# A two-layer hybrid block on one core: the dt projection as fp32 matmuls in four column groups, the row of norm factors built later, eleven warm-up matmuls for nine

## The chip, the cores and the metric

The kernel runs on one core of a Trainium2 chip. The metric is the time of one execution in microseconds (us), the median of several. PE is TensorE (PEld its weight loads), DVE is VectorE, ACT is ScalarE, POOL is GpSimd, SP is the engine that issues most DMAs.

## The reference

Two layers work on x, [256 tokens, 1024]. Each layer norms x, multiplies it by an input matrix, and runs three branches (a gated spatial mixer, a state space scan, a differential attention) that are gated, merged and projected; a feed forward part follows. What matters here is the norm and the small product `ssm_dt`, 16 columns of the input matrix:

```python
h = rmsnorm(x, attn_norm_g[layer])          # x / rms(x) by token, times a gain by feature
proj = h @ w_in[layer]
gm_u, gm_v, ssm_z, ssm_xbc, ssm_dt, da_q, da_k, da_v, gates = split_cols(proj, IN_SIZES)
...
dt = softplus(ssm_dt.astype(float32) + dt_bias.astype(float32))   # [256, 16]
```

dt sets the decays of the scan, so it is needed with full fp32 precision.

## The kernel before

x stays in SBUF as `x_sb`, features on partitions: 8 tiles of [128 features, 256 tokens], fp32. The gain is multiplied in at once (`scaled_tile`, L353), and the result is kept as two parts in the fp32r format, `h_hi` and `h_lo`. The factor of a token, 1 / rms, is applied later to what the products give. All large weights come as one stream of blocks [128, 2048] (`raw`, 1 MB); each half block is split into `whi` (ACT, L231) and `wlo` (DVE, L234), up to four halves ahead of use (`AHEAD`). Each product is three matmuls (`mm3`, L274): high by high, high by low, low by high. Products with 512 output columns go through `tok_group` (L302; q, k, v, the spatial gate, z, the branch gates), products with features on partitions through `feat_half` (L280; x B C, u, and the feed forward). The items follow each other in the order of `MIX`, q first, then k, then x4, x5 (the pairs of tiles of B and C) and so on.

Beside the stream run generators that `tick` (L257) advances, once for each half block. Two of them matter here:

- `norm_factors` (L366) squares x, sums over features with matmuls against ones (`an_ss`, L382), takes the inverse root on POOL (`an_r`, `an_rp`, L322 and L324), then spreads the factors along a row with matmuls against the identity (`an_rb`, L389) and copies that row to `an_row` (L393). `an_rp` (by token on partitions) scales q and k (L443) and others; `an_row` is first used for x4 (`normed`, L678). The layer finishes this generator between q and k (L449).
- `dt_raw` (L466) multiplies h by the 16 dt columns. The weights are kept as `ws`, [128, 8 tiles, 128 columns] in fp32r: 16 columns of high parts, 16 of low parts, 96 of zeros. `layer_constants` (L404) makes it: a memset on POOL (L419), a DMA from SP that waits for the memset (L420), a copy on ACT (L422), a subtraction on DVE (L423). Sixteen matmuls (L470) take `h_hi` and `h_lo` of the 8 tiles as the moving operand and give `pd`; rows 0 to 31 of it are copied to `dT` (L472) and turned by two matmuls with a stacked identity (`pdt`, L477), which add the two halves.

A scheduler sets the order in which the instructions of an engine stand; each engine runs its own in that order. fp32r matmuls of 128 columns of weights are one instruction with one record of the trace; an fp32 matmul leaves two records, one behind the other. A few bf16 matmuls on zeros (`warm`, L170, nine of them) run before the first data is there.

Of the kernel before, what the change touches and what calls it, by code (L numbers as in the profile page):

```python
# [11 lines left out]
F32 = mybir.dt.float32  # L12
# [18 lines left out]
# order of the mixer's input products: q, k, v, spatial gate g, u, x B C in pairs of tiles, z  # L31
MIX = ("q", "k", "x4", "x5", "v", "x0", "x1", "z0", "x2", "x3", "z1", "g", "u0", "u1")
# buffers of 4 KiB, of 2 KiB and of the split weights
NS4, NS2, NWB, AHEAD = 18, 7, 5, 4
HP = 200
# feed forward: hidden tile after which the down products start
LAG = 5
CUM_WAIT = 6
WARM = 9
# [4 lines left out]
# columns of w_in  # L44
# [3 lines left out]
# row constants of a layer  # L48
R_GMG, R_GMB, R_SSG, R_DTB, R_D, R_QK, R_SUB = 0, 512, 1024, 2048, 2064, 2080, 2208
R_N = 2336  # L50
# per-partition constants of a layer
PC_CW, PC_CB, PC_FW, PC_FB = 0, 48, 60, 60 + 6 * NFT
PC_N = PC_FB + 2 * NFT
# gains of the input norms, per layer: mixer, feed forward
G_N = 16
# constants that depend on shapes alone
# [5 lines left out]
def feat_block(w, c0, c1):  # L62
    """[1024, cols c0:c0+128 and c1:c1+128] -> [128, 2 tiles, 8 k, 128]"""
    a = w.reshape(8, P, -1)
    return np.stack([a[:, :, c : c + P].transpose(1, 0, 2) for c in (c0, c1)], 1).reshape(P, BLK)


def tok_blocks(w):
    """[K, 512 n] -> blocks of [128, 4 k, 512], the k halves of a column group together"""
    k, n = w.shape  # L70
    a = w.reshape(k // 512, 4, P, n // 512, 512).transpose(3, 0, 2, 1, 4)
    return list(a.reshape(-1, P, BLK))


def out_blocks(w):
    """[1024, 1024] -> blocks of [128, 4 tiles, 4 k, 128], halves of k outermost"""
    a = w.reshape(2, 4, P, 2, 4, P).transpose(0, 3, 2, 4, 1, 5)
    return list(a.reshape(-1, P, BLK))
# [41 lines left out]
def bc(ap, n):  # L120
    """append a broadcast dim of n"""
    return ap.unsqueeze(len(ap.shape)).to_broadcast([*ap.shape, n])
# [3 lines left out]
def block_kernel(ctx: ExitStack, tc: tile.TileContext, x, wstream, wdt, rows, prol, pcols, gains, gmw, consts, out):  # L126
# [20 lines left out]
    # the residual stream, features on partitions  # L147
# [13 lines left out]
    # the activation table is there before the data  # L161
# [3 lines left out]
    # the tensor engine's clock is up when the data comes  # L165
# [16 lines left out]
    def prologue():  # L182
        """lambda and -exp(a_log) of both layers"""
        nc.sync.dma_start(pr, prol.rearrange("(o l) f -> o l f", o=1).to_broadcast([P, L, 272]))
        for l in range(L):
            lv = pr[:, l, 0:256].rearrange("p (a b d) -> p a b d", a=2, b=2)
            nc.vector.tensor_tensor(lprod[:, 2 * l : 2 * l + 2, :], lv[:, :, 0, :], lv[:, :, 1, :], op=ALU.mult)
        nc.vector.tensor_reduce(lsum.rearrange("p l a -> p (l a)"), lprod, op=ALU.add, axis=AX.X)
        nc.scalar.activation(lexp, lsum, AF.Exp)
        nc.scalar.activation(aneg, pr[:, :, 256:272], AF.Exp)  # L190
        nc.vector.tensor_scalar(aneg, aneg, -1.0, None, op0=ALU.mult)
        nc.vector.tensor_tensor(neglam, lexp[:, :, 1], lexp[:, :, 0], op=ALU.subtract)
        for l in range(L):
            lam_init = 0.8 - 0.6 * math.exp(-0.3 * l)
            nc.vector.tensor_scalar(neglam[:, l : l + 1], neglam[:, l : l + 1], -lam_init, None, op0=ALU.add)

# [5 lines left out]
    def load_half():  # L202
        i, hf = divmod(stream["i"], 2)
        parts = 1
        if hf == 0:
            raw = wpool.tile([P, BLK], F32, tag="raw", name=f"raw{i}", bufs=3)
            if i == 0:
                # the first block and the tiles of x as they are needed
                for q in range(4):
                    cs = slice(q * 512, (q + 1) * 512)  # L210
                    nc.sync.dma_start(x_sb[:, 2 * q : 2 * q + 2, :], x[:, 2 * q : 2 * q + 2, :])
                    nc.sync.dma_start(raw[:, cs], wstream[i, :, cs])
            elif i == 1:
                for q in range(2):
                    cs = slice(q * HB, (q + 1) * HB)
                    nc.sync.dma_start(raw[:, cs], wstream[i, :, cs])
                nc.sync.dma_start(cst, consts)
            else:
                nc.sync.dma_start(raw, wstream[i])
# [18 lines left out]
    def next_half():  # L238
        """the next half block; those after it are split ahead"""
# [6 lines left out]
    def load_table(name):  # L246
        """the next activations in program order, with their table set in place"""
        table["ins"] = tc.keep_in_program_order(nc.scalar.preload_act_table_set(name)).ins

# [24 lines left out]
    def mm3(o, a_hi, a_lo, b_hi, b_lo, start, stop):  # L274
        """o += a.T @ b, operands as high + low parts of 12 bits"""
# [4 lines left out]
    def feat_half(o, h_hi, h_lo):  # L280
        """one tile of 128 features of h @ w, features on partitions: o [128, 256]"""
# [6 lines left out]
    def feat_pair(o, h_hi, h_lo):  # L288
        """two tiles, with the last features of h as late as can be"""
# [12 lines left out]
    def tok_group(name, act, nk, evac, between=None):  # L302
        """512 columns of a product, tokens on partitions: act(k, i) gives the high and low
        activations of token tile i, evac(i, psum) takes what comes out"""
# [14 lines left out]
    def rsqrt_mean(src, n, scale, name):  # L319
        """(src * scale + eps) ** -0.5"""  # L320
# [15 lines left out]
    def transpose_split(src, dst, name, nk, scale=1.0):  # L336
        """src [128 tokens, nk * 128] -> features on partitions, high and low parts;
        dst(k0, k1) gives where tiles k0 to k1 go"""
# [14 lines left out]
    def scaled_tile(k, g, h_hi, h_lo):  # L353
        """feature tile k of x times its gain, split; the norm's factor of a token is applied to
        what the products give"""
# [10 lines left out]
    def norm_factors(name, res):  # L366
        """1 / rms of x by token: res gets [128, 2] with tokens on partitions, half of it, and the
        same along a row"""
# [17 lines left out]
        yield  # L386
# [7 lines left out]
        rh = sm.tile([P, 2], F32, tag="rhalf", name=f"{name}_rh", bufs=2)  # L394
        nc.vector.tensor_scalar(rh, r[:, 0:2], 0.5, None, op0=ALU.mult)
        res.update(r=r, rh=rh, row=row)
# [7 lines left out]
    def layer_constants(l):  # L404
        if l == 0:
# [12 lines left out]
        wd = s4(f"wd{l}", [P, 8, P])  # L418
        nc.gpsimd.memset(wd, 0.0)  # L419
        nc.sync.dma_start(wd[:, :, 0:HEADS], wdt[l])  # L420
        ws = s4(f"ws{l}", [P, 8, P], F32R)
        nc.scalar.activation(ws, wd, AF.Copy)  # L422
        nc.vector.tensor_tensor(  # L423
            ws[:, :, HEADS : 2 * HEADS], wd[:, :, 0:HEADS], ws[:, :, 0:HEADS].bitcast(F32), op=ALU.subtract
# [6 lines left out]
    for l in range(L):  # L431
# [15 lines left out]
        nf_side = add_side(norm_factors(f"an{l}", nf), 1)  # L447
        tok_group(f"q{l}", h_act, 8, evac_qk(0))
        finish(nf_side)  # L449
        r_in, rh_in, row_in = nf["r"], nf["rh"], nf["row"]  # L450
# [15 lines left out]
        def dt_raw():  # L466
            pd = ps(f"pd{l}")
            for k in range(8):
                for m, part in enumerate((h_hi, h_lo)):
                    nc.tensor.matmul(pd[:, 0:S], ws[:, k, :], part[:, k, :], start=k + m == 0, stop=k + m == 8)  # L470
            dT = sm.tile([2 * HEADS, S], F32, tag="acT", name=f"dT{l}", bufs=1)
            nc.vector.tensor_copy(dT, pd[0 : 2 * HEADS, 0:S])  # L472
# [3 lines left out]
            for i in range(2):  # L476
                nc.tensor.matmul(  # L477
                    pdt[:, 16 * i : 16 * i + 16], dT[:, i * P : (i + 1) * P], cst[0 : 2 * HEADS, K_II : K_II + HEADS],
# [8 lines left out]
            # one table set for both functions  # L487
# [3 lines left out]
            # softplus(x) = max(x, 0) + log1p(exp(-|x|))  # L491
# [8 lines left out]
            # what rounding 1 + e dropped, to first order  # L500
# [10 lines left out]
            # cumulative sums within chunks: by token, by head, and what is left to the end of chunk 0  # L511
# [63 lines left out]
        def attention():  # L575
# [17 lines left out]
            def soft(h):  # L593
                # columns: (tile 0, map 0), (tile 0, map 1), (tile 1, map 0), (tile 1, map 1)
# [18 lines left out]
            def combine(h):  # L613
                # weights over sum 0: p0 - lam * (sum0 / sum1) * p1
# [60 lines left out]
        def normed(o, row, name):  # L675
            """two feature tiles times the norm's factors"""
# [43 lines left out]
        def conv(u, y, wcol, bcol, taps, pcl):  # L720
            """causal depthwise convolution along the free axis"""
# [13 lines left out]
        def ssd_in():  # L735
            # B with tokens on partitions
# [7 lines left out]
            # C B^T, lower triangle, transposed  # L744
# [12 lines left out]
        def x_tokens(b):  # L757
            """half the heads with tokens on partitions: x, dt x, the skip term, and what chunk 0
            leaves to chunk 1"""
# [39 lines left out]
        def xbc_block(j):  # L799
# [3 lines left out]
            u = normed(o, row_in, f"cu{l}_{j}")  # L803
# [15 lines left out]
        def ssd():  # L819
# [13 lines left out]
            def decay(i, g):  # L833
                # exp(min(a_t - a_s, 0))
# [61 lines left out]
        def u_block(j):  # L896
# [3 lines left out]
            u = normed(o, row_in, f"uu{l}_{j}")  # L900
# [16 lines left out]
        # what can go beside the stream once these items are there  # L917
# [9 lines left out]
        for item in MIX[1:]:  # L927
            items[item[0]](int(item[1:] or 0))
            done.add(item)
# [13 lines left out]
        # a gate is (tanh(x / 2) + 1) / 2; the half is taken where the merged sum is split  # L943
# [70 lines left out]
        nf_side = add_side(norm_factors(f"fn{l}", nff), 1)  # L1014
# [59 lines left out]
def shape_constants():  # L1074
# [3 lines left out]
    c[: 2 * HEADS, K_II : K_II + HEADS] = np.concatenate([np.eye(HEADS)] * 2)  # L1078
# [80 lines left out]
```

## Time and profile before

| | us |
|---|---|
| median of 3 runs | 973.7 |
| lowest and highest run | 973.24, 974.42 |
| span of the profiled execution, first to last instruction | 970.6 |
| PE busy in the span | 961.9 (99%) |
| DVE, ACT, POOL busy | 714.7, 572.9, 39.3 |

The page gives the span of the profiled execution, not its whole time; 3.1 us lie between that span and the median of the runs. A row of the timeline reads: start in us, us until the end of the last instruction of the row, engine, line of the kernel, operation, out<-in with the shape, how many, and in brackets the idle time before it and what ended it. Matmuls overlap each other in it: what one costs is the distance from its start to the next one's start (its pitch), not its duration.

### The profile page before, as it was taken

What the parts mean: (1) busy time and instruction counts of PE and PEld (TensorE: products, weight loads), DVE (VectorE), ACT (ScalarE), POOL (GpSimd) and SP (SyncE); (2) the same over time, 40 slices, a digit from 0 to 9 for tenths busy, and PEclk for the clock granted to TensorE, in tenths of its full rate; (3) what the DMA queues carried; (4) which work ended last, traced back from release to release, by engine and by line L of the source; (5) the groups of instructions that cost most, each with busy time, mean ns of one, the idle gap of its engine ahead of it and who ended that gap; (6) DMA issues with size and microseconds to landing.
All of it is one profiled execution on the core that took longest, in us unless ns stands there. A gap on an engine that the chain in (4) does not pass through costs nothing.

```text
span 970.6 us, 15931 instructions
## 1 busy us (share of the span) xinstructions
PE 961.9 (99%) x6465; PEld 877.5 (90%) x6465; DVE 714.7 (74%) x1072; ACT 572.9 (59%) x880; POOL 39.3 (4%) x48
## 2 busy tenths in 40 slices
PE   8999999999999999999999999999999999999998
PEld 5999787888899999999988988878888999999998
DVE  6698767667568978787677975776756788877774
ACT  6676577554445755555457666776544566555552
POOL 2020010000000000000001100000000000000000
PEclk9999999999999999999999999999999999999999
DMA  7854572347555555555544555633455545555541
GB/s 294 277 178 174 174 260 99 131 141 243 186 174 174 175 187 194 184 177 177 190 177 151 175 175 174 234 113 131 158 189 175 178 169 198 193 175 177 186 160 44
DMA packets 29145, 172.71 MB, mean 178 GB/s; under 512 B 5232, under 2 KB 6544, under 8 KB 9360
## 3 DMA queue, kind: packets, MB, share of 16 engines
q1 hardware_dynamic: 27712, 167.46, 49.9%
q0 software_dynamic: 1216, 4.23, 1.4%
q8 instruction: 50, 0.82, 0.3%
q14 instruction: 23, 0.19, 0.1%
q10 hardware_dynamic: 144, 0.02, 0.0%
HBM read 170.61 MB, written 1.08 MB: 177 GB/s over the span
## 4 chain that ended last, share of the span: by engine, by line
PE 98%; DMA 0%; POOL 0%; ACT 0%; DVE 0%; issue 0%; ACTq 0%; POOLq 0%
PE up L276 9%; PE up L277 9%; PE up L278 9%; PE acc L278 4%; PE acc L277 4%; PE acc L276 4%; PE xbc L276 2%; PE xbc L277 2%; PE xbc L278 2%; PE sc L587 2%; PE wo L278 2%; PE wo L277 2%; PE wo L276 2%; PE g_a L276 2%; PE g_a L277 2%; PE g_a L278 2%
## 5 line engine op out<-in xcount | busy, mean ns | idle before, releaser
L231 ACT ACTIVATE whi<-raw 128x1024 fp32r<-128x1024 f32 (+1 forms) x310 | 325.0, 1051 | 274.8 <-PE up L277 82.4
L234 DVE TENSOR_TENSOR wlo<-raw,whi 128x1024 fp32r<-128x1024 f32 (+1 forms) x310 | 375.8, 1216 | 148.1 <-ACT whi L231 145.5
L276 PE MATMUL up<-f_hi,whi 128*128 128x256 f32 x704 | 199.6, 283 | 0.0
L277 PE MATMUL up<-f_lo,whi 128*128 128x256 f32 x704 | 199.2, 283 | 0.0
L278 PE MATMUL up<-f_hi,wlo 128*128 128x256 f32 x704 | 199.2, 283 | 0.0
L277 PEld LDWEIGHTS up<-f_lo,whi 128*128 128x128 f32 x704 | 135.2, 192 | 0.0
L276 PEld LDWEIGHTS up<-f_hi,whi 128*128 128x128 f32 x704 | 135.2, 192 | 0.0
L278 PEld LDWEIGHTS up<-f_hi,wlo 128*128 128x128 f32 x704 | 135.1, 192 | 0.0
L276 PE MATMUL acc<-act,whi 128*128 128x256 f32 x352 | 99.6, 283 | 0.0
L277 PE MATMUL acc<-act,whi 128*128 128x256 f32 x352 | 99.6, 283 | 0.0
L278 PE MATMUL acc<-act,wlo 128*128 128x256 f32 x352 | 99.6, 283 | 0.0
L727 DVE SCALAR_TENSOR_TENSOR fy<-fu,pc,fy 128x254 f32<-128x254 f32 (+1 forms) x176 | 73.6, 478 | 0.2
L276 PEld LDWEIGHTS acc<-act,whi 128*128 128x128 f32 x352 | 67.6, 192 | 0.0
L277 PEld LDWEIGHTS acc<-act,whi 128*128 128x128 f32 x352 | 67.6, 192 | 0.0
L278 PEld LDWEIGHTS acc<-act,wlo 128*128 128x128 f32 x352 | 67.6, 192 | 0.0
L276 PE MATMUL xbc<-h_hi,whi 128*128 128x256 f32 x192 | 55.1, 287 | 0.0
L277 PE MATMUL xbc<-h_lo,whi 128*128 128x256 f32 x192 | 54.3, 283 | 0.0
L278 PE MATMUL xbc<-h_hi,wlo 128*128 128x256 f32 x192 | 54.3, 283 | 0.0
L722 ACT ACTIVATE fy<-fu,pc 128x256 f32<-128x256 f32 x88 | 47.7, 588 | 3.8 <-DVE fu L678 3.8
L328 ACT ACTIVATE act<-fy 128x256 fp32r<-128x256 f32 x44 | 18.3, 416 | 49.3 <-DVE fy L1023 49.3
L678 DVE TENSOR_TENSOR fu<-up,fn_row 128x512 f32<-128x512 f32 x44 | 30.2, 690 | 16.0 <-PE up L278 16.0
L277 PEld LDWEIGHTS xbc<-h_lo,whi 128*128 128x128 f32 x192 | 36.8, 192 | 0.1
(305 smaller groups left out, 1970.9 us busy)
## 6 DMA issues: line engine op xcount, KB each, us to landing
raw<-in_wstream SPq DMA_DIRECT2D x152, 1024.0 KB, 4.9
seg<-scr POOLq DMA_DIRECT2D x8, 512.0 KB, 7.0
rows<-in_rows SPq DMA_DIRECT2D x2, 1168.0 KB, 7.9
x_sb<-in_x SPq DMA_DIRECT2D x4, 256.0 KB, 4.5
raw<-in_wstream SPq DMA_DIRECT2D x4, 256.0 KB, 4.7
raw<-in_wstream SPq DMA_DIRECT2D x2, 512.0 KB, 6.7
out_x<-x_sb SPq DMA_DIRECT2D x8, 128.0 KB, 1.8
gmw<-in_gmw SPq DMA_DIRECT2D x2, 256.0 KB, 6.0
```

The source lines that it names most:

```text
L231: split = nc.scalar.activation(hi[:, cs], src[:, cs], AF.Copy)
L234: nc.vector.tensor_tensor(lo[:, cs], src[:, cs], hi[:, cs].bitcast(F32), op=ALU.subtract)
L276: nc.tensor.matmul(o, a_hi, b_hi, start=start, stop=False)
L277: nc.tensor.matmul(o, a_hi, b_lo, start=False, stop=False)
L278: nc.tensor.matmul(o, a_lo, b_hi, start=False, stop=stop)
L328: nc.scalar.activation(dst_hi, src, AF.Copy, scale=scale)
L587: nc.tensor.matmul(o[:, c0 : c0 + n], qT[ms, h, i * P : (i + 1) * P], kT[ms, h, 0:n], start=True, stop=False)
L678: nc.vector.tensor_tensor(u, o.rearrange("p (m t) -> p m t", m=2), row.unsqueeze(1).to_broadcast([P, 2, S]), op=ALU.mult)
L722: nc.scalar.activation(y, u, AF.Identity, bias=pcl[:, bcol : bcol + 1], scale=pcl[:, wcol + taps - 1 : wcol + taps])
L727: nc.vector.scalar_tensor_tensor(y[:, d:], u[:, : S - d], pcl[:, w : w + 1], y[:, d:], op0=ALU.mult, op1=ALU.add)
```

## The change

The dt weights are kept as fp32, [128, 8, 32] with 16 columns of zeros, in a buffer of their own; the gain of the norm is multiplied into them. The product takes `x_sb` itself as the moving operand, in fp32: eight matmuls of 32 weight columns, tile k = 2q + kk to rows 32q to 32q + 31 of `pd`, so that two tiles are summed in each of four groups of PE columns. The copy `dT` has 128 rows, and the matmuls `pdt` add the four groups with a longer stacked identity. `norm_factors` gives out `r` and `rh` before the row, and waits `later` steps before it builds the row: 4 in the mixer (before 1), 1 in the feed forward (as before). The layer no longer finishes the generator between q and k, but after k. `WARM` is 11.

```diff
-WARM = 9
+ROW_WAIT = 4
+WARM = 11
...
-    def norm_factors(name, res):
+    def norm_factors(name, res, later):
...
         r = rsqrt_mean(ss, 2, 1.0 / D, f"{name}_r")
-        yield
+        rh = sm.tile([P, 2], F32, tag="rhalf", name=f"{name}_rh", bufs=2)
+        nc.vector.tensor_scalar(rh, r[:, 0:2], 0.5, None, op0=ALU.mult)
+        res.update(r=r, rh=rh)
+        for _ in range(later):
+            yield
         t2 = ps(f"{name}_rb")
...
-        res.update(r=r, rh=rh, row=row)
+        res.update(row=row)
...
-        wd = s4(f"wd{l}", [P, 8, P])
-        nc.gpsimd.memset(wd, 0.0)
-        nc.sync.dma_start(wd[:, :, 0:HEADS], wdt[l])
-        ws = s4(f"ws{l}", [P, 8, P], F32R)
-        nc.scalar.activation(ws, wd, AF.Copy)
+        ws = lpool.tile([P, 8, 2 * HEADS], F32, tag="ws", name=f"ws{l}", bufs=1)
+        nc.gpsimd.memset(ws, 0.0)
+        nc.sync.dma_start(ws[:, :, 0:HEADS], wdt[l])
         nc.vector.tensor_tensor(
-            ws[:, :, HEADS : 2 * HEADS], wd[:, :, 0:HEADS], ws[:, :, 0:HEADS].bitcast(F32), op=ALU.subtract
+            ws[:, :, 0:HEADS], ws[:, :, 0:HEADS], bc(gcol[:, l * G_N : l * G_N + 8], HEADS), op=ALU.mult
         )
...
-        nf_side = add_side(norm_factors(f"an{l}", nf), 1)
+        nf_side = add_side(norm_factors(f"an{l}", nf, ROW_WAIT), 1)
         tok_group(f"q{l}", h_act, 8, evac_qk(0))
-        finish(nf_side)
-        r_in, rh_in, row_in = nf["r"], nf["rh"], nf["row"]
+        r_in, rh_in = nf["r"], nf["rh"]
...
             pd = ps(f"pd{l}")
-            for k in range(8):
-                for m, part in enumerate((h_hi, h_lo)):
-                    nc.tensor.matmul(pd[:, 0:S], ws[:, k, :], part[:, k, :], start=k + m == 0, stop=k + m == 8)
-            dT = sm.tile([2 * HEADS, S], F32, tag="acT", name=f"dT{l}", bufs=1)
-            nc.vector.tensor_copy(dT, pd[0 : 2 * HEADS, 0:S])
+            for kk in range(2):
+                for q in range(4):
+                    k = 2 * q + kk
+                    nc.tensor.matmul(
+                        pd[32 * q : 32 * q + 32, 0:S], ws[:, k, :], x_sb[:, k, :], start=kk == 0, stop=kk == 1
+                    )
+            dT = sm.tile([P, S], F32, tag="acT", name=f"dT{l}", bufs=1)
+            nc.vector.tensor_copy(dT, pd[:, 0:S])
...
-                    pdt[:, 16 * i : 16 * i + 16], dT[:, i * P : (i + 1) * P], cst[0 : 2 * HEADS, K_II : K_II + HEADS],
+                    pdt[:, 16 * i : 16 * i + 16], dT[:, i * P : (i + 1) * P], cst[:, K_II : K_II + HEADS],
...
             items[item[0]](int(item[1:] or 0))
+            if item == "k":
+                finish(nf_side)
```

How the instructions stand on the engines changes at these places. PE in layer 0, at the end of q and the start of k, before (`q_1`, `k_0`, `k_1` are the outputs of q and k for the two halves of the tokens; whi and wlo the parts of a half block):

```order
L278 MATMUL q_1_111<-whi_1_157,h_lo 128x512
L389 MATMUL an_rb<-cst,an_rp 128x128 x2
L276 MATMUL k_0_295<-whi_0_163,h_hi 128x512
L276 MATMUL k_1_296<-whi_0_163,h_hi 128x512
L277 MATMUL k_0_295<-wlo_0_164,h_hi 128x512
```

PE at the same place, as changed:

```order
L279 MATMUL q_1_113<-whi_1_159,h_lo 128x512
L277 MATMUL k_0_290<-whi_0_165,h_hi 128x512
L277 MATMUL k_1_291<-whi_0_165,h_hi 128x512
L278 MATMUL k_0_290<-wlo_0_166,h_hi 128x512
L279 MATMUL k_0_290<-whi_0_165,h_lo 128x512
```

k now follows q with nothing between them. PE further into k, as changed (the third half block of k has the high part `whi_0_211`, the fourth `whi_1_238`):

```order
L277 MATMUL k_1_291<-whi_0_211,h_hi 128x512
L474 MATMUL pd_310<-x_sb,ws_267 32x256 x8
L278 MATMUL k_1_291<-wlo_0_212,h_hi 128x512
L279 MATMUL k_1_291<-whi_0_211,h_lo 128x512
L277 MATMUL k_1_291<-whi_0_211,h_hi 128x512
L278 MATMUL k_1_291<-wlo_0_212,h_hi 128x512
L279 MATMUL k_1_291<-whi_0_211,h_lo 128x512
L394 MATMUL an_rb<-cst,an_rp 128x128 x2
L483 MATMUL pdt_360<-cst,dT_319 128x16 x2
L277 MATMUL k_0_290<-whi_1_238,h_hi 128x512
```

The matmuls of `an_rb` have left the seam between q and k and stand behind `pd`, in the third half block of k; the seven matmuls of that half ahead of `pd` were eleven before. In layer 1 they move in the same way, there `pd` stands behind the first half of k (as before) and `an_rb` with `pdt` behind the third.

DVE in layer 0, as changed, from the split of the second half block of k on (`an_rh` is half of `an_rp`, `subg` a constant, `dtx` and `dtn` the first steps of softplus, `wlo_0_295` the first half block of x4):

```order
L235 TENSOR_TENSOR wlo_1_194<-raw_163,whi_1_193 128x1024
L388 TENSOR_SCALAR an_rh<-an_rp 128x2
L235 TENSOR_TENSOR wlo_0_212<-raw_209,whi_0_211 128x1024
L235 TENSOR_TENSOR wlo_1_239<-raw_209,whi_1_238 128x1024
L420 TENSOR_SCALAR subg_265<-rows_260 128x128
L425 TENSOR_TENSOR ws_267<-ws_267,gcol 128x8x16
L478 COPY dT_319<-pd_310 128x256
L398 COPY an_row<-an_rb 128x256
L488 SCALAR_TENSOR_TENSOR dtx_273<-pdt_360,an_rp,rows_260 128x16 x2
L499 SCALAR_TENSOR_TENSOR dtn_392<-dtx_273 128x32
L235 TENSOR_TENSOR wlo_0_295<-raw_292,whi_0_294 128x1024
```

`an_row` stood ahead of `an_rh` before and now stands behind `dT`; both `dtx` and `dtn` now stand ahead of `wlo_0_295`, where before one `dtx` did. On POOL the memset of `ws` moves from behind `an_rp` to the start of the program, ahead of everything that waits; on SP the DMA of the dt weights of layer 1 moves from the end of layer 0 to its start, behind the DMA of `pc` for layer 1.

## Rows read from the trace of the kernel before

**Rows 1.** The page: the span, the busy times of the engines, and the chain that ended last by engine.

```profile
span 970.6 us, 15931 instructions
PE 961.9 (99%) x6465; PEld 877.5 (90%) x6465; DVE 714.7 (74%) x1072; ACT 572.9 (59%) x880; POOL 39.3 (4%) x48
PE 98%; DMA 0%; POOL 0%; ACT 0%; DVE 0%; issue 0%; ACTq 0%; POOLq 0%
```

**Rows 2.** The longest of the waits of PE: the engine and line that waited, what ended it, us in total, times, the longest.

```profile
PE an_rb L389 <- POOL an_rp L324: 2.6, 2, 2.3
```

**Rows 3.** The timeline of layer 0 from the end of q to the start of x4, PE.

```profile
19.19 0.40 PE L278 MATMUL q<-whi,h_lo 128*128 128x512 f32 x1
21.87 0.71 PE L389 MATMUL an_rb<-cst,an_rp 128*128 128x128 f32 x4 [2.29 <-POOL an_rp L324]
22.34 0.71 PE L276 MATMUL k<-whi,h_hi 128*128 128x512 f32 x2
...
30.17 0.39 PE L277 MATMUL k<-wlo,h_hi 128*128 128x512 f32 x1
30.40 0.28 PE L470 MATMUL pd<-h_hi,ws 128*128 128x256 f32 x1
...
32.31 0.40 PE L278 MATMUL k<-whi,h_lo 128*128 128x512 f32 x1
...
36.06 0.28 PE L276 MATMUL xbc<-h_hi,whi 128*128 128x256 f32 x1
```

**Rows 4.** The timeline of the same stretch, POOL, ACT and DVE.

```profile
20.24 1.57 POOL L324 TENSOR_TENSOR an_rp<-an_r,mhalf 128x2 f32<-128x2 f32 x1
21.85 1.27 ACT L443 ACTIVATE qk<-q,an_rp 128x512 f32<-128x512 f32 x2 [4.24 <-POOL an_rp L324]
23.00 2.01 ACT L231 ACTIVATE whi<-raw 128x1024 fp32r<-128x1024 f32 x2
18.88 2.36 DVE L234 TENSOR_TENSOR wlo<-raw,whi 128x1024 fp32r<-128x1024 f32 x2
24.09 2.36 DVE L234 TENSOR_TENSOR wlo<-raw,whi 128x1024 fp32r<-128x1024 f32 x2
26.37 0.22 DVE L417 TENSOR_SCALAR subg<-rows 128x128 f32<-128x128 f32 x1
27.83 0.29 DVE L423 TENSOR_TENSOR ws<-wd,ws 128x128 fp32r<-128x128 f32 x1 [1.24 <-ACT ws L422]
32.51 0.41 DVE L472 COPY dT<-pd 32x256 f32<-32x256 f32 x1 [4.39 <-PE pd L470]
```

**Rows 5.** Matmuls in fp32, two records each. From the timeline, one of 512 columns with full width; from the view of its tile the duration of one record (ns: shortest, median, longest); from the timeline two of `cum`, of which L515 has 16 weight columns and 128 moving ones; from its tile's view the weight load of L515.

```profile
96.85 1.02 PE L787 MATMUL st<-xde,btok 128*128 128x512 f32 x2
...
L787 PE MATMUL st<-xde,btok x8: 590/591/592, 96.8 to 601.6; 128*128 128x512 f32 x8
...
53.91 0.39 PE L515 MATMUL cum<-cst,dta 128*16 128x128 f32 x2
54.23 0.40 PE L516 MATMUL cum<-dta,cst 128*128 128x16 f32 x2
...
L515 PEld LDWEIGHTS cum<-cst,dta x8: 92/94/96, 53.3 to 532.8; 128*16 128x16 f32 x8
```

**Rows 6.** The timeline of layer 1, PE: `an_ss`, the wait for `an_rb`, and `pdt`, with neighbours.

```profile
498.15 0.58 PE L382 MATMUL an_ss<-ones,an_sq 128*128 128x1 f32 x4
498.59 0.49 PE L278 MATMUL q<-whi,h_lo 128*128 128x512 f32 x1
...
500.79 0.71 PE L389 MATMUL an_rb<-cst,an_rp 128*128 128x128 f32 x4 [0.32 <-POOL an_rp L324]
...
511.26 0.39 PE L278 MATMUL k<-whi,h_lo 128*128 128x512 f32 x1
511.57 0.61 PE L477 MATMUL pdt<-cst,dT 32*128 32x16 f32 x4
512.12 0.50 PE L276 MATMUL k<-whi,h_hi 128*128 128x512 f32 x1
```

**Rows 7.** The timeline of the start, PE, and DVE's split of the third half block of q.

```profile
1.18 4.02 PE L170 MATMUL warm<-cold 128*128 128x512 bf16 x9 [1.18 <-DVE cold L167]
5.90 1.22 PE L276 MATMUL q<-whi,h_hi 128*128 128x512 f32 x2 [0.71 <-ACT whi L231]
...
9.48 0.63 PE L277 MATMUL q<-wlo,h_hi 128*128 128x512 f32 x1
9.91 0.54 PE L278 MATMUL q<-whi,h_lo 128*128 128x512 f32 x1
10.29 0.40 PE L277 MATMUL q<-wlo,h_hi 128*128 128x512 f32 x1
10.53 0.40 PE L278 MATMUL q<-whi,h_lo 128*128 128x512 f32 x1
...
13.96 0.39 PE L277 MATMUL q<-wlo,h_hi 128*128 128x512 f32 x1
...
12.18 1.23 DVE L234 TENSOR_TENSOR wlo<-raw,whi 128x1024 fp32r<-128x1024 f32 x1 [0.98 <-ACT whi L231]
```

**Rows 8.** Two stretches of 4 us, in layer 0 and at the same work in layer 1: busy time by engine, then the granted clock (1.00 is 2.4 GHz), DMA share, GB/s.

```profile
160.00:164.00 4.00, 4.00 (x14) 2.77 (x13) 4.00 (x8) 2.20 (x7) 0.92 (x1) 0.57 0.56 231
644.00:648.00 4.00, 4.00 (x19) 2.64 (x18) 3.53 (x4) 3.69 (x10) 0.00 (x0) 1.00 0.02 4
```

More of the change, by code (lines that the diff above doesn't have):

```diff
@@ L393, in norm_factors @@
         nc.vector.tensor_copy(row, t2[:, 0:S])
-        rh = sm.tile([P, 2], F32, tag="rhalf", name=f"{name}_rh", bufs=2)
-        nc.vector.tensor_scalar(rh, r[:, 0:2], 0.5, None, op0=ALU.mult)
-        res.update(r=r, rh=rh, row=row)
+        res.update(row=row)
     def hT_pair(name):
@@ L802, in xbc_block @@
                 feat_half(o[:, m * S : (m + 1) * S], h_hi, h_lo)
-            u = normed(o, row_in, f"cu{l}_{j}")
+            u = normed(o, nf["row"], f"cu{l}_{j}")
             y = s2(f"cv{l}_{j}", [P, 2, S])
@@ L899, in u_block @@
                 feat_half(o[:, m * S : (m + 1) * S], h_hi, h_lo)
-            u = normed(o, row_in, f"uu{l}_{j}")
+            u = normed(o, nf["row"], f"uu{l}_{j}")
             nc.scalar.activation(uT[:, 2 * j : 2 * j + 2, :], u, AF.Gelu_apprx_tanh)
@@ L1013, in block_kernel @@
         nff = {}
-        nf_side = add_side(norm_factors(f"fn{l}", nff), 1)
+        nf_side = add_side(norm_factors(f"fn{l}", nff, 1), 1)
         def up_out(j, o):
@@ L1077, in shape_constants @@
     r = np.arange(P)
-    c[: 2 * HEADS, K_II : K_II + HEADS] = np.concatenate([np.eye(HEADS)] * 2)
+    c[:, K_II : K_II + HEADS] = np.concatenate([np.eye(HEADS), np.zeros((HEADS, HEADS))] * 4)
     c[:, K_TRI : K_TRI + P] = r[:, None] <= r[None, :]
```

## The prediction

> **What bounds the kernel now.** I read the page first: PE is busy 961.9 of 970.6 us, and 98% of the chain that ended last is PE [rows 1]. So the other engines cost something only where PE waits for them, and the list of PE's waits is short: 2.6 us in all, nearly all of it one wait of 2.3 us for `an_rp` [rows 2]. The rest is PE's own work: a matmul of 512 columns takes 0.23 us from its start to the next start (30.17 to 30.40) [rows 3]. The timeline of layer 0 shows the wait: q's last matmul starts at 19.19, `an_rb` at 21.87, since the inverse root on POOL runs from 20.24 to 21.81 [rows 3, 4]. Layer 1 waits 0.32 us at the same place [rows 6]. The change touches PE at three places: that seam, the product `pd` behind it, and the start.
>
> **The seam in layer 0.** PE would be free at 19.19 + 0.23 = 19.42 and stands idle for 2.29 us [rows 3]. With `an_rb` behind `pd`, k follows q at once. What is late next? k's first half needs its low part: DVE splits two halves from 18.88 in 2.36 us, so the first is there at 20.06; PE issues two matmuls on the high part (to 19.88) and waits 0.2 us. Ten matmuls then last to 22.4, the second half (its split ends at 21.24) to 25.1. The third half hangs on the chain that stopped PE before: ACT's scaled copies of q wait for `an_rp` to 21.85, behind them the high part starts at 23.00, the low part at 24.09 and is there at 25.27 [rows 4]. PE starts that half with a matmul on the high part, to 25.3: this just holds. After seven matmuls, at 26.7, stands `pd`, which needs `ws`: DVE ends the splits at 26.45 and `subg` at 26.59, then multiplies `ws`, 0.29 us by the subtraction of the same shape [rows 4], to 26.9: 0.2 us. So of 2.29 us some 0.4 come back: **-1.85 us**. Behind `pd` DVE runs `dT`, `an_row`, `dtx` twice and `dtn` ahead of x4's first split; PE meanwhile has five matmuls of k, `an_rb`, `pdt` and twelve more of k, 17 x 0.23 + 0.9 = 4.8 us. DVE's chain is bound by `an_rb` and `pdt`, 2 us behind the end of `pd`, then 0.8 us of small work and 1.2 us of split: 4.0 us. No wait for x4, with 0.8 us to spare; if that cover were gone PE would wait by what is missing, as it would for `pdt` if `dT` (0.41 us [rows 4]) were over 1 us late.
>
> **The seam in layer 1.** 0.32 us of wait [rows 6]; three halves now stand between. **-0.3 us**.
>
> **The product.** Removed: 16 matmuls from 30.40 to 32.31, 1.91 us [rows 3], in both layers. Added: eight fp32 matmuls of 256 columns, two records each. Two records of 512 columns end 1.02 us after the start, and one lasts 0.591 [rows 5]: 0.43 us apart, so 0.215 for 256 columns. No row shows two matmuls in different column groups, so how far the groups run beside each other is the unknown. Upper bound, one behind the other: 16 x 0.215 = 3.44 us, +1.5 a layer. Lower bound, all four beside each other: two rounds of two records, 0.86 us, -1.05 a layer. I take the middle: the records come as group 0, 0, 1, 1, 2, 2 and so on; the two of one group must follow each other, as the two of `st` do, and the second runs beside the first of the next group. That makes 1 + 7 + 1 = 9 steps, 1.94 us: **0**. The Trainium skill, in TensorE: Matmul & The Clock Gate, Part 3 (What overlaps and what doesn't), says that matmuls start and end strictly in program order even in different tiles; by that rule the sum is this one and not the lower bound.
>
> The groups also mean a change of the shape in use. `cum` with 16 weight columns takes 0.32 us for two records of 128 columns (53.91 to 54.23), where 2 x 0.215 / 2 would be 0.215 [rows 5]: 0.1 us, and I charge it on the way in and out, in two layers: **+0.4** (bounds 0 and +0.8). TensorEngine Tiling (Array Packing) of the Trainium skill, Key Properties, says that changing the mode drains the engine; it gives no price, so the row's stands. `pdt` gets full height: now 512.12 - 511.26 - 0.23 = 0.63 us, the equally full `an_ss` 0.44 (498.15 to 498.59) [rows 6], so **-0.4** in two layers (bounds 0 and -0.4). The smaller memset, ACT's dropped copy and the extra table load of ACT in layer 0 cost nothing: PE reaches x5, the first half behind that load, some 10 us after `pd`, and its split is through some 8 us after `pd`. On SP the DMA of layer 1's weights now passes the block transfers of layer 0's start; its memset is done by then, and blocks are split four halves ahead, so nothing waits.
>
> **The warm-up.** Nine bf16 matmuls end at 5.20, PE idles 0.71 us, and q starts at 5.90 [rows 7]. Then a matmul of 512 columns takes 0.43 us (9.48 to 9.91), the level of 1.2 GHz; from 10.29 on 0.24, that of 2.4 GHz [rows 7]. Two more at 0.43 fill the idle time, so q starts no later, and PE has worked without a gap since 1.18 instead of 5.90; I expect the rise, which came at about 10.1 after that idle time, to come before or early in q. But q is then held by its data: the third half's low part is there at 12.18 + 1.23 = 13.41, and PE used it at 13.96 [rows 7]. So at most 0.55 us; **-0.4** (bounds 0 and -0.55).
>
> Sum: -1.85 - 0.3 + 0 + 0.4 - 0.4 - 0.4 = -2.55 us, 968.05 for this span. The median of the runs lies 3.1 us above the span; I leave that as it is: 973.7 - 2.6 = **971.1 us**. About 0.2%, 1.95 us, is what can be told from no change.
>
> **The rivals.**
> - *All four groups beside each other.* For it: `pd` is ordered so that four matmuls in a row go to four groups. Against it: both records of a matmul stand together. -2.55 - 2 x 1.08 = -4.7, 969.0. The skill's tiling page (TensorEngine Tiling, Key Properties) says that tiles load and multiply in parallel; that rule alone would give this time. No run here shows it.
> - *One group after the other.* For it: every fp32 record of the trace follows the one before it. -2.55 + 2 x 1.5 = +0.45, 974.1. The faster seam pays for a slower product.
> - *Slower: one after the other with the weight load in the open.* The load of 16 columns takes 94 ns [rows 5]; if it hides behind nothing when the group changes, a record costs 0.215 + 0.094, `pd` 16 x 0.309 = 4.94 us, +3.0 a layer: -2.55 + 6.0 = +3.5, 977.2. It ends on the slower side once `pd` takes 1.94 + (2.55 + 1.95) / 2 = 4.2 us in a layer. Against it: full loads hide behind matmuls all over this trace.
> - *The wait comes back.* The same `an_rp` holds ACT, hence k's third half, and I found no slack there: if that chain ends 1.85 us later than I work out, PE waits in the third half instead: -2.55 + 1.85 = -0.7, 973.0.
>
> Beside these, the clock: in layer 0 the granted clock is 0.57 in 160 to 164 and 1.00 at the same work of layer 1 [rows 8]: 0.43 x 4 us = 1.7 us of work at 2.4 GHz are lost. The work there is moved in time by 2 us; the dip may vanish, or layer 1 may get one. I take that as 1.7 us either way with small weight, in the range.
>
> **The numbers.** Chances: the forecast 0.45 (its own range 970.0 to 972.2), all beside each other 0.15, one after the other 0.27, loads in the open 0.07, the wait back 0.06. Faster by over 0.2% means below 971.75: 0.36 of the forecast's 0.45, all of the second, 0.03 of the third, 0.54. Slower means above 975.65: 0.06 of the fourth, 0.02 of the third with a dip, 0.08. Between them 0.38. The range of 8 in 10 reaches from 968.5 (the second case, without its faster tail) to 975.0 (the third, with 0.9 for the drains); the fourth is left out.
>
> **What the profile will show.** Right: no wait of PE at `an_rb`; k's first matmul at about 19.4 or, with the early clock, 19.0; `pd` from its first start to the next k matmul about 2.1 us; q's matmuls at 0.23 before 9 us. Wrong: `pd` near 1 us or at 3.4 us and more; a new wait of over 0.5 us for `whi`, `wlo` or `ws` in k; q's pitch at 0.43 to 10 us as before.

## The result and the profile after

The changed kernel takes 966.94 us, the kernel before 974.06 us on the same chip: a ratio of 0.9926, interval 0.9912 to 0.9940. That is 7.1 us or 0.7% faster. The forecast was 971.1 us with a range down to 968.5, so the time lies outside it. One execution of the kernel before, in `before_again`, took 5356.53 us; it stands in no ratio, median or count below. The profiled execution took 967.21 us, its span is 964.9 us; against the span of before [rows 1] that is 5.7 us less.

The page: span, busy times of the engines, and the chain that ended last.

```profile
span 964.9 us, 15932 instructions
PE 958.5 (99%) x6467; PEld 872.1 (90%) x6467; DVE 714.0 (74%) x1072; ACT 572.1 (59%) x879; POOL 38.2 (4%) x48
PE 98%; DMA 1%; DVE 0%; ACT 0%; issue 0%; SPq 0%
```

PE is still 98% of the chain. Its waits, the whole list:

```profile
PE warm L171 <- DVE cold L168: 1.2, 1, 1.2
PE q L278 <- DVE wlo L235: 0.4, 1, 0.4
PE q L277 <- ACT whi L232: 0.4, 1, 0.4
```

The wait at `an_rb`, 2.6 us in [rows 2], is gone, and no wait of more than 0.3 us stands in k. The timeline of PE in layer 0, which answers to [rows 3]:

```profile
19.78 0.40 PE L279 MATMUL q<-whi,h_lo 128*128 128x512 f32 x1
20.01 0.62 PE L277 MATMUL k<-whi,h_hi 128*128 128x512 f32 x2
20.75 0.50 PE L278 MATMUL k<-wlo,h_hi 128*128 128x512 f32 x1
...
27.23 0.39 PE L277 MATMUL k<-whi,h_hi 128*128 128x512 f32 x1
27.55 1.07 PE L474 MATMUL pd<-x_sb,ws 128*32 128x256 f32 x16
28.55 0.50 PE L278 MATMUL k<-wlo,h_hi 128*128 128x512 f32 x1
...
29.83 0.60 PE L394 MATMUL an_rb<-cst,an_rp 128*128 128x128 f32 x4
30.27 0.52 PE L483 MATMUL pdt<-cst,dT 128*128 128x16 f32 x4
30.64 0.48 PE L277 MATMUL k<-whi,h_hi 128*128 128x512 f32 x1
...
33.45 0.28 PE L277 MATMUL xbc<-h_hi,whi 128*128 128x256 f32 x1
```

Three things are to be seen. First, k's first matmul starts one pitch behind q's last (19.78 to 20.01), where 2.29 us lay idle before; the split of the weights then holds the third matmul for 0.28 us (20.75 instead of 20.01 + 2 x 0.23). Second, `pd` takes from 27.23 + 0.23 = 27.46 to 28.55, **1.09 us** instead of 1.91 [rows 3]. Third, `an_rb` and `pdt` now stand side by side and cost 30.64 - 29.83 = 0.81 us together, where `an_rb` alone took 0.47 (21.87 to 22.34 [rows 3]) and `pdt` alone 0.63 (layer 1 [rows 6]): 0.29 less. Which of the two got cheaper, and by what, `groups_only` shows below. From the end of q to x4 it is 13.44 us instead of 16.64, 3.20 less: 2.29 - 0.28 + 0.82 + 0.29 = 3.12 of it are named.

Layer 1, which answers to [rows 6]:

```profile
495.92 0.39 PE L279 MATMUL q<-whi,h_lo 128*128 128x512 f32 x1
496.14 0.39 PE L277 MATMUL k<-whi,h_hi 128*128 128x512 f32 x1
...
498.63 0.39 PE L279 MATMUL k<-whi,h_lo 128*128 128x512 f32 x1
498.95 1.07 PE L474 MATMUL pd<-x_sb,ws 128*32 128x256 f32 x16
499.95 0.50 PE L277 MATMUL k<-whi,h_hi 128*128 128x512 f32 x1
...
509.19 0.28 PE L277 MATMUL xbc<-h_hi,whi 128*128 128x256 f32 x1
```

No wait, and `pd` again 1.09 us. From q's first matmul to x4 layer 1 went from 26.14 to 24.50 us, 1.64 less; 0.32 + 0.82 + 0.29 = 1.43 of it are named.

The start, which answers to [rows 7]:

```profile
1.18 4.88 PE L171 MATMUL warm<-cold 128*128 128x512 bf16 x11 [1.18 <-DVE cold L168]
5.92 0.80 PE L277 MATMUL q<-whi,h_hi 128*128 128x512 f32 x1
...
7.15 0.39 PE L279 MATMUL q<-whi,h_lo 128*128 128x512 f32 x1
7.38 0.39 PE L277 MATMUL q<-whi,h_hi 128*128 128x512 f32 x1
...
10.22 0.73 PE L277 MATMUL q<-whi,h_hi 128*128 128x512 f32 x2 [0.41 <-ACT whi L232]
...
13.14 1.23 DVE L235 TENSOR_TENSOR wlo<-raw,whi 128x1024 fp32r<-128x1024 f32 x1 [0.85 <-ACT whi L232]
```

The pitch is 0.23 us from 7.15 on (0.43 before, up to 10 us), but nothing comes of it: q waits for its data, which came later in this execution (the low part of the third half at 13.14 instead of 12.18), and q ends 0.59 us later than before. In the windows of this stretch the granted clock reads 1.00 in all profiles, whatever the pitch, so here the pitch has to stand for it: 0.43 us is also the pitch inside the half-clock stretch of before (162.47 to 162.90 us).

The windows that answer to [rows 8] show the granted clock of both layers at 1.00 (last but two):

```profile
156.00:160.00 4.00, 4.00 (x21) 2.66 (x21) 4.00 (x10) 2.99 (x8) 1.54 (x1) 1.00 0.74 256
640.00:644.00 4.00, 4.00 (x19) 2.64 (x19) 3.71 (x9) 2.67 (x9) 0.00 (x0) 1.00 0.09 14
```

The stretch at half clock of before is gone: ahead of it the same work stands 2.6 us earlier than before, behind it 4.1, so 1.5 us come from it. The two spans then differ by +0.6 (start) - 3.2 (layer 0) - 1.5 (clock) - 1.6 (layer 1) = -5.7 us, all of it found. The last 1.4 us to the 7.1 of the medians lie in the other executions, and that is what the experiments on the clock are about.

### The profile page after: what moved, and what is told of

Read it like the earlier page. It is cut to its first block, busy times and chain, and to the rows that moved or that the text cites. A ratio compares the mean times of both kernels' runs of the same rounds, so it can differ in the third digit from the quotient of the medians.

```text
span 964.9 us, 15932 instructions
## 1 busy us (share of the span) xinstructions
PE 958.5 (99%) x6467; PEld 872.1 (90%) x6467; DVE 714.0 (74%) x1072; ACT 572.1 (59%) x879; POOL 38.2 (4%) x48
## 3 DMA queue, kind: packets, MB, share of 16 engines
HBM read 170.61 MB, written 1.08 MB: 178 GB/s over the span
## 4 chain that ended last, share of the span: by engine, by line
PE 98%; DMA 1%; DVE 0%; ACT 0%; issue 0%; SPq 0%
PE up L277 9%; PE up L278 9%; PE up L279 9%; PE acc L279 4%; PE acc L277 4%; PE acc L278 4%; PE xbc L277 2%; PE xbc L279 2%; PE xbc L278 2%; PE sc L593 2%; PE wo L278 2%; PE wo L277 2%; PE wo L279 2%; PE g_a L277 2%; PE z L279 2%; PE g_c L277 2%
```

## The experiments

The mean granted clock of an execution tells how many stretches at half clock it holds: one loses some 1.7 us of 970, so 0.999 to 1.000 is none, 0.997 to 0.998 one, 0.995 to 0.996 two, 0.994 three. The fourteen profiles agree: those of `before`, `before_again` and `groups_only`, for example, have 0.998, 0.996 and 0.994 and show one, two and three stretches. The slow pitch at the start isn't in this mean (`warm_nine` has it, at 1.000). Number of executions, with the median time in us:

| kernel | none | one | two | three |
|---|---|---|---|---|
| before (80 executions, three chips) | 0 | 33: 973.16 | 47: 974.79 | 0 |
| changed (first comparison and `after_again`) | 6: 967.17 | 3: 968.46 | 0 | 0 |
| `warm_only` | 0 | 6: 973.4 | 5: 975.1 | 0 |
| `wait_filled` | 9: 972.08 | 2: 973.7 | 0 | 0 |
| `groups_only` | 3: 970.2 | 2: 971.2 | 3: 972.9 | 4: 974.5 |
| `row_early` | 2: 969.8 | 3: 971.55 | 4: 972.95 | 3: 974.0 |
| `padded_product` | 4: 968.9 | 1: 970.0 | 0 | 0 |
| `group_inner` | 4: 967.1 | 1: 968.2 | 1: 970.6 | 0 |
| `warm_nine` | 1: 966.9 | 4: 968.5 | 0 | 0 |
| `two_groups` | 1: 969.4 | 3: 970.8 | 1: 972.55 | 0 |
| `one_group` | 6: 972.6 | 5: 973.7 | 0 | 0 |
| `thin_filled` | 6: 971.2 | 1: 971.8 | 0 | 0 |

### The kernel before and the changed kernel once more

> The kernel before, unchanged, to learn whether the stretch of half clock at 160 to 164 us belongs to it. Theory A (the stretch belongs to this order of work): the profile shows it again within 1 us of the same place, it costs about 1.7 us, and all runs stay within 1 us of 974. Theory B (it is chance, present in some executions): the profile has none or has it elsewhere, and runs with and without it differ by about 1.7 us.

Measured: 974.57 us, ratio 1.0004 (0.9995 to 1.0012). The windows of its profile (granted clock last but two):

```profile
18.00:22.00 4.00, 1.97 (x11) 1.36 (x9) 2.67 (x4) 0.34 (x1) 2.47 (x2) 0.98 0.74 305
22.00:26.00 4.00, 3.74 (x12) 3.23 (x13) 2.38 (x4) 3.40 (x5) 2.35 (x3) 0.59 0.41 58
160.00:164.00 4.00, 4.00 (x21) 2.66 (x21) 4.00 (x9) 2.99 (x8) 1.41 (x1) 1.00 0.80 277
640.00:644.00 4.00, 4.00 (x15) 3.08 (x14) 2.96 (x6) 2.24 (x7) 0.00 (x0) 0.61 0.44 184
```

Here 160 to 164 us is at full clock; the clock is down at the end of the wait for `an_rp` and after it (PE busy 1.97 of 4 us, then a clock of 0.59) and in the work of layer 1 that corresponds to [rows 8]. Neither theory is quite right: two profiles show three places, and by their mean clock all 80 executions of before get one or two stretches, never none. That a second one costs 974.79 - 973.16 = 1.6 us agrees with a clock of 0.59 over 4 us (1.6 us lost).

> The changed kernel, unchanged, for more executions. Seen so far in the kernel before: each half-clock stretch costs about 1.6 us, and its executions hold one (mean clock 0.998) or two (0.996) of them, at 22, 160 and 640 us. Theory A (the change takes the stretches away): all executions at 0.999 or 1.0 and within 1 us of 967. Theory B (chance): of some ten executions several at 0.998 or lower and at 968.5 or more.

Measured: 968.27 us, ratio 0.9937 (0.9925 to 0.9949). Theory A falls: three of five executions hold one stretch, at 968.3 to 968.6. But over both comparisons six of nine hold none, against 0 of 80 before.

### Filling the wait

```diff
         yield
+        if name == "an0":
+            fill = ps("fill")
+            for _ in range(8):
+                nc.tensor.matmul(fill, cold[:, 0:P], cold, start=True, stop=True)
         t2 = ps(f"{name}_rb")
```

> The kernel before with eight bf16 matmuls of 512 columns on zeros put into PE's wait for an_rp in layer 0; their result isn't used. They last 8 x 0.23 = 1.84 us of the 2.29 us and move nothing else. Theory A (the half-clock stretch at 22 us follows that idle time): it can't come, so executions at 0.996 give way to ones at 0.998 and some at 1.0, and the median falls from 974.4 by 0.8 to 1.6 us. Rival (the stretch has another cause, or the others come whatever is done here): the same mix of 0.996 and 0.998, and 974.4.

Measured: 972.18 us, ratio 0.9984 (0.9976 to 0.9993). PE's timeline, then two windows:

```profile
19.50 0.40 PE L278 MATMUL q<-whi,h_lo 128*128 128x512 f32 x1
19.74 1.90 PE L390 MATMUL fill<-cold 128*128 128x512 bf16 x8
22.18 0.71 PE L393 MATMUL an_rb<-cst,an_rp 128*128 128x128 f32 x4 [0.54 <-POOL an_rp L324]
22.65 0.48 PE L276 MATMUL k<-whi,h_hi 128*128 128x512 f32 x1
```

```profile
18.00:22.00 4.00, 3.64 (x19) 1.99 (x17) 2.58 (x4) 0.42 (x1) 2.55 (x2) 1.00 0.76 306
22.00:26.00 4.00, 3.82 (x19) 3.23 (x20) 2.78 (x4) 3.38 (x5) 2.30 (x3) 1.00 0.36 46
```

`an_rb` comes no sooner (22.18, 2.68 us behind q's last matmul, as before), and yet the kernel is 1.6 to 1.9 us faster: nine of eleven executions hold no stretch at half clock. So the idle wait cost its 2.3 us and, in most executions, stretches at half clock on top. Theory A holds, and more came than it explains: all five profiles of kernels with the idle wait (two of before, `warm_only`, `groups_only`, `row_early`) have a stretch at 160 or at 640 us, and two of them one at 22 us too; with the wait filled only two of eleven executions have any. Over the whole table 110 of 115 executions with the idle wait hold a stretch, and 22 of 59 without it, among these 5 of 11 of `one_group` and 4 of 5 of `warm_nine`. So the wait makes the stretches more frequent; it is not their only cause.

### The parts of the change, one by one

`warm_only` is the kernel before with more warm-up alone:

```diff
-WARM = 9
+WARM = 11
```

> The kernel before with 11 instead of 9 warm-up matmuls, nothing else. Theory of the prediction: q's pitch is 0.23 us from about 7 us on, but data holds q, so 0 to -0.55 us. Rival (the start gives nothing, since both low parts of q's third half come when they come): 0.0, within 0.3. If the half-clock stretch in layer 0 hangs on when work comes rather than on the padded product, it may vanish here: then -1.7 more.

Measured: 973.79 us, ratio 1.0001 (0.9992 to 1.0010). The rival holds: more warm-up gives nothing that can be told. `warm_nine` is the other side, the same lines the other way round in the changed kernel:

> The changed kernel with 9 warm-up matmuls instead of 11. Theory now (q is held by its data, and when the clock rises differs between executions anyway): within 0.3 us of the changed kernel where neither holds a half-clock stretch. Theory of the prediction: +0.4 us, since the clock rises later in q.

Measured: 968.34 us, ratio 0.9944 (0.9931 to 0.9958); its one execution without a stretch takes 966.9, the changed kernel's 967.17. Its start, and then that of the kernel before, run again, both with nine:

```profile
7.57 0.63 PE L279 MATMUL q<-whi,h_lo 128*128 128x512 f32 x1
7.99 0.63 PE L278 MATMUL q<-wlo,h_hi 128*128 128x512 f32 x1
8.42 0.63 PE L279 MATMUL q<-whi,h_lo 128*128 128x512 f32 x1
```

```profile
7.09 0.39 PE L278 MATMUL q<-whi,h_lo 128*128 128x512 f32 x1
7.32 0.40 PE L277 MATMUL q<-wlo,h_hi 128*128 128x512 f32 x1
```

With the same nine matmuls the pitch at 7 to 8.5 us is 0.43 in one execution and 0.23 in the other. The span of `warm_nine` is 964.6 us all the same: how early the pitch falls differs between executions, and q waits for its data either way. Over all fourteen profiles q's last matmul starts at 19.0 to 20.6 us, and the three with the slow pitch to 9.5 us and later (19.19, 19.38, 19.50) are among the first five.

`groups_only`: the four column groups, `ws` in 32 columns and `pdt` at full height in the kernel before.

```diff
-                    nc.tensor.matmul(pd[:, 0:S], ws[:, k, :], part[:, k, :], start=k + m == 0, stop=k + m == 8)
+                        pd[32 * q : 32 * q + 32, 0:S], ws[:, k, :], x_sb[:, k, :], start=kk == 0, stop=kk == 1
```

> The kernel before with the fp32 product in four column groups alone; the row factors and the warm-up stay as before. Theory now: pd costs 1.09 us instead of 1.91 in both layers (-1.64), pdt 0.26 less (-0.5), so -2.1 us: 971.9, and the wait of 2.3 us for an_rp stays. Theory of the prediction (records of one group in a row, nine steps): 0 for pd, -0.1 in all. If the half-clock stretch was tied to the padded product, 1.7 more in both cases.

Measured: 972.80 us, ratio 0.9984 (0.9972 to 0.9995). Theory now had 971.9; the median lies among the executions with two stretches. Without a stretch it is 970.2, 1.9 us below `wait_filled` without one (972.08), which has the same seam: 2.1 was expected. PE at `pdt` in layer 1, with `an_rb` still between q and k:

```profile
511.42 0.39 PE L278 MATMUL k<-whi,h_lo 128*128 128x512 f32 x1
511.65 0.51 PE L478 MATMUL pdt<-cst,dT 128*128 128x16 f32 x4
512.01 0.48 PE L276 MATMUL k<-whi,h_hi 128*128 128x512 f32 x1
```

At full height `pdt` takes 512.01 - 511.42 - 0.23 = 0.36 us by itself, instead of 0.63 with 32 rows [rows 6]. So 0.27 of the 0.29 us come from its shape, and next to nothing from `an_rb` beside it. `padded_product`, which follows, shows the other side: there `an_rb` and `pdt` of 32 rows stand side by side in layer 1 and take 1.08 us (506.74 to 507.82), and 0.47 + 0.63 = 1.10 apart.

`padded_product`: the padded product in the changed kernel.

```diff
-        ws = lpool.tile([P, 8, 2 * HEADS], F32, tag="ws", name=f"ws{l}", bufs=1)
+        wd = s4(f"wd{l}", [P, 8, P])
+        ws = s4(f"ws{l}", [P, 8, P], F32R)
...
-                        pd[32 * q : 32 * q + 32, 0:S], ws[:, k, :], x_sb[:, k, :], start=kk == 0, stop=kk == 1
+                    nc.tensor.matmul(pd[:, 0:S], ws[:, k, :], part[:, k, :], start=k + m == 0, stop=k + m == 8)
```

> The changed kernel with the padded, split product put back; later row factors and 11 warm-up matmuls stay. Theory now: it keeps -1.9 to -2.3 us of the seams and loses the 2.1 us of the groups: about 969.1 if the half-clock stretch stays away, 970.8 if it comes back. Theory of the prediction: the product is worth nothing, 967 to 967.5.

Measured: 969.36 us, ratio 0.9950 (0.9938 to 0.9962). Without a stretch 968.9 against 967.17: the product is worth 1.8 us, from this side too. That the product is worth nothing is refuted.

`row_early`: the row factors between q and k again, in the changed kernel.

```diff
-ROW_WAIT = 4
+ROW_WAIT = 1
...
         tok_group(f"q{l}", h_act, 8, evac_qk(0))
+        finish(nf_side)
```

> The changed kernel with the row factors broadcast between q and k again, as before; fp32 groups and 11 warm-up matmuls stay. Theory now: the wait of some 2.3 us comes back, the seams lose 2.0 to 2.3 us, and half-clock stretches come back in some executions: 969 with none, 970.6 with one, 972.2 with two. Theory of the prediction: +2.15 for the seams and nothing else, 969.1, in all executions.

Measured: 972.89 us, ratio 0.9985 (0.9974 to 0.9995). The first of PE's waits in its trace:

```profile
PE an_rb L394 <- POOL an_rp L325: 2.6, 2, 2.3
```

The wait is back, and with it the stretches at half clock: ten of twelve executions hold one to three. Without one it takes 969.8, 2.7 us more than the changed kernel; the seams (2.29 - 0.28 + 0.32) make 2.3, and 0.4 stay unexplained: `pdt` has its full height here too (0.35 us in layer 1, 510.69 to 511.27 less 0.23), so the place of `an_rb` costs next to nothing.

### How the column groups run

`group_inner`: the loops over `q` and `kk` exchanged.

```diff
-            for kk in range(2):
-                for q in range(4):
+            for q in range(4):
+                for kk in range(2):
```

> The changed kernel with the two matmuls of a column group issued one after the other (groups 0 0 1 1 2 2 3 3 instead of 0 1 2 3 0 1 2 3). If a record starts beside the last one only when their groups differ, and program order holds, the first records of neighbours can't go beside each other: four records of one group in a row, the last beside the first of the next group, 4 + 3 + 3 + 3 = 13 steps of 0.215, pd 2.8 us instead of 1.09, +3.4 us in two layers: 970.4. If the array lets waiting groups start whatever the order, pd stays at 1.1 us: 966.9.

Measured: 967.23 us, ratio 0.9937 (0.9924 to 0.9951).

```profile
27.37 0.40 PE L277 MATMUL k<-whi,h_hi 128*128 128x512 f32 x1
27.70 1.09 PE L474 MATMUL pd<-x_sb,ws 128*32 128x256 f32 x16
28.72 0.50 PE L278 MATMUL k<-wlo,h_hi 128*128 128x512 f32 x1
```

27.60 to 28.72, 1.12 us. The new order did reach the engine: in the trace the first records of the four groups start at 27.699, 27.712, 27.725 and 27.739 us, 13 ns apart with one more matmul issued between each two, against 7 ns in the changed kernel (27.547 to 27.567). So the order of issue hardly matters: a matmul of the next group starts although one of the group before, issued ahead of it, still waits for its predecessor. The sentence on the kernel before, that each engine runs its instructions in the order in which they stand, does not hold among these matmuls.

`one_group` and `two_groups`: the eight matmuls in one sum on rows 0 to 31, or in two of four each; the groups' rows of `dT` that are left are set to zero.

```diff
-                        pd[32 * q : 32 * q + 32, 0:S], ws[:, k, :], x_sb[:, k, :], start=kk == 0, stop=kk == 1
+                nc.tensor.matmul(pd[0:32, 0:S], ws[:, k, :], x_sb[:, k, :], start=k == 0, stop=k == 7)
```

> The changed kernel with all eight fp32 matmuls of pd in one column group of 32, one sum; a memset of dT on POOL is added for the rows that the groups no longer fill. Theory now (a group runs its records one after the other, other groups beside it, plus 0.23 us for going in and out): 16 x 0.215 + 0.23 = 3.67 us instead of 1.09 in each layer, +5.2 us. Theory that 32 columns of fp32 are cheap by themselves, whatever the groups: 1.1 us, no change.

Measured: 972.95 us, ratio 0.9988 (0.9980 to 0.9997).

```profile
26.46 0.39 PE L277 MATMUL k<-whi,h_hi 128*128 128x512 f32 x1
26.78 3.64 PE L474 MATMUL pd<-x_sb,ws 128*32 128x256 f32 x16
30.35 0.50 PE L278 MATMUL k<-wlo,h_hi 128*128 128x512 f32 x1
```

> The changed kernel with the eight matmuls of pd in two column groups, four in each (memset of dT on POOL as with one group). Theory now: 8 x 0.215 + 0.23 = 1.95 us in each layer, +1.7 us. Rival (a second group is not free, each record of it costs its issue and part of its stream): between 2.2 and 3.4 us.

Measured: 970.84 us, ratio 0.9966 (0.9954 to 0.9979).

```profile
27.37 0.39 PE L277 MATMUL k<-whi,h_hi 128*128 128x512 f32 x1
27.68 1.92 PE L476 MATMUL pd<-x_sb,ws 128*32 128x256 f32 x16
29.54 0.50 PE L278 MATMUL k<-wlo,h_hi 128*128 128x512 f32 x1
```

From the end of the matmul ahead to the next one of k: 26.69 to 30.35, 3.66 us, and 27.60 to 29.54, 1.94 us; both as expected (3.67 and 1.95). With 1.09 for four groups that is a straight line: 0.215 us for each record that a group runs (16, 8 and 4), and 0.23 once, for going in and out. In whole times, each without a stretch, one group costs 5.5 us more than the changed kernel (5.2 expected), two groups 2.2 from a single execution (1.7 expected).

### The thin products

```diff
                 ty[i, g] = ps(f"y{l}_{i}_{g}")
+                for _ in range(4 if (i, g) == (0, 0) else 0):
+                    nc.tensor.matmul(ty[i, g], cold[:, 0:P], cold, start=True, stop=True)
...
                     o = ps(f"sc{l}_{h}_{m}")
+                    for _ in range(2 if h == 2 else 0):
+                        nc.tensor.matmul(o, cold[:, 0:P], cold, start=True, stop=True)
```

> The changed kernel with eight bf16 matmuls of 512 columns on zeros put into the stretch of thin products (gm, y, sc) of each layer, four ahead of y and two ahead of each sc of the third head; their result is overwritten. They cost 8 x 0.23 = 1.84 us a layer, 3.7 us. Theory A (the half-clock stretches at 160 and 640 us follow the thin products): all executions at 0.999 or 1.0, 970.7 without spread. Rival (they follow something else): one execution in three keeps a stretch, at 972 and more.

Measured: 971.18 us, ratio 0.9969 (0.9959 to 0.9980). Six of seven executions hold no stretch, the seventh has 0.998 and 971.8. The median without one is 4.0 us above the changed kernel, for 3.7 expected. That speaks for theory A, but the changed kernel is without a stretch in six of nine too, so seven executions don't settle it. As a remedy the filling costs more than it can bring.

## Why the prediction was wrong

Take the steps in turn.

- **Seam of layer 0, -1.85**: right. 2.29 us of wait went, 0.28 came back: -2.01. The 0.2 that I charged for `ws` did not come.
- **Seam of layer 1, -0.3**: right, 0.32 is gone.
- **The product, 0**: this step failed. I wrote that the records come as group 0, 0, 1, 1 and that "the two of one group must follow each other", nine steps and 1.94 us. That the two of one group follow each other is right, and `one_group` shows it; what does not follow is that the next group waits for it. Each group runs its own records, and four groups run beside each other: their first records start within 0.02 us (27.547 to 27.567), and they take four rounds of 0.215. That makes -0.82 in each layer, -1.64 in all, and `pd` near 1 us (27.55 to 28.55), which I had named as a sign of being wrong. I took the step from the Trainium skill's rule of strict program order (TensorE: Matmul & The Clock Gate, Part 3, What overlaps and what doesn't). For these fp32 matmuls in column groups `group_inner` speaks against it: strict order makes 2.8 us, 1.12 were measured. The other rule that I weighed, that tiles multiply in parallel (the Trainium skill, TensorEngine Tiling (Array Packing), Key Properties), agrees: 3.66, 1.94 and 1.09 us for one, two and four groups.
- **Shape of the array, +0.4**: right in size; 0.23 us for each `pd` is the constant of the line, and it is contained in the 1.09.
- **`pdt`, -0.4**: right, and somewhat more. Its full height is worth 0.27 in each layer (`groups_only`), and `an_rb` and `pdt` together take 0.29 less.
- **Warm-up, -0.4**: wrong, it is 0 within 1 us (`warm_only`), and the profiles show why: q is held by its data.
- **The list of PE's waits**, which I read as 2.6 us in all: it is longer, 4.5 us, with 1.2 ahead of the warm-up and 0.7 ahead of q. Neither bears on the seams.
- **"The median of the runs lies 3.1 us above the span; I leave that as it is"**, with 1.7 us for the clock either way and small weight: this step failed too. The profiled execution held one stretch at half clock, at 160 us; the median of before holds one or two. No execution of before is without one, so a baseline without any is an estimate: 971.5 (973.16 - 1.63) or 972.1 (`wait_filled`), and the changed kernel's is 967.2. So the work got faster by 4.4 to 4.9 us, and 2.2 to 2.7 of the measured 7.1 are stretches that no longer come. The parts read from the traces agree: -2.01 - 0.32 - 1.64 - 0.58 = -4.55, where I had -2.55.

The rival in which all groups run beside each other forecast -4.7 us of work: that was the mechanism and the size, and I gave it 0.15. Even its 969.0 missed, because it too kept the clock of before.

What stays open: which execution gets which stretch. That the idle wait brings more stretches at half clock is shown by filling it and by bringing it back; why kernels without it hold some too was not found. That the falls at 160 and 640 us follow the thin products is argued from where they lie and only supported by `thin_filled`; how filling a wait at 20 us also thins out the stretches there, and why no execution of before is without any, was not found.

## What to carry to other kernels

Small fp32 products can be cheaper in column groups: here their price is the longest group's records one behind the other, plus 0.23 us once, whatever the order of issue. A small fp32 matmul with few rows can gain from standing at full height: `pdt` fell from 0.63 to 0.36 us. An idle wait of PE of some two microseconds can cost again behind its end, by a stretch at half clock, so removing it, or only filling it with matmuls on zeros, can bring more than the wait itself. Before summing against a median, read the granted clock of each execution: the profiled one may hold another number of such stretches than the median does.

## What was unexpected of the hardware

- Matmuls of different column groups start past a waiting one: 1.12 us for eight in either order of issue, against 3.66 in one group.
- In one of the two profiles of before the wait of 2.29 us is followed by 4 us at a mean granted clock of 0.59; with 1.90 us of matmuls on zeros in it the clock stays at 1.00 in the one profile taken, and the kernel gets 0.16% faster (0.07 to 0.24) although `an_rb` comes no sooner.
- When the pitch falls to 0.23 us at the start differs between executions with the same nine warm-up matmuls: it is 0.43 in one and 0.23 us in another at 8 us.
- The same small fp32 matmuls take less with 128 rows than with 32: 0.36 against 0.63 us.
